# The first pass turned round: tokens stationary, split weights moving, results a token to a partition

## The chip, the cores and the metric

The kernel runs on one core of a Trainium2 chip. TensorE multiplies a stationary operand of at most 128 x 128, which it loads first, by a moving operand of up to 512 columns, and adds into a PSUM bank. VectorE (DVE), ScalarE (ACT) and GpSimd (POOL) do the work beside it, and 16 DMA engines, most of whose transfers SyncE (SP) starts, bring the weights from HBM. The metric is the device time of one execution in microseconds (us). The kernel before takes 3499.53 us (median of three runs, 3499.0 to 3501.36).

## The reference

The program computes one layer of a block on 512 tokens of 2048 channels: a norm, one combined projection, two branches (forgetting attention and multi-scale pooling), a gated merge, and then a retrieval of single-neuron experts.

```python
h = rms_norm(x, norm1_g)                              # x: 512 x 2048
q, k, v, fl, pin, gl = split(h @ w_in)                # 1024 1024 1024 8 1024 4096 columns
log_f = log_sigmoid(fl + forget_bias)
attn = forgetting_attention(rms(q), rms(k), v, log_f) # 8 heads x 128, causal
# pooling: trailing mean over 2, 4, 8 or 16 tokens minus the token itself, then a 256 x 256 map
merged = sig(gl_A) * (attn @ w_branch_attn) + sig(gl_B) * (pool * scale @ w_branch_pool)
x = x + merged @ w_out
xn = rms_norm(x, norm2_g)
s1, s2 = (xn @ w_query) @ sub_keys                    # 8 heads, 2 halves, 128 keys each
# top 16 of s1, top 16 of s2, top 16 of the 256 sums -> 16 experts a head and token
x = x + sum over the experts of gelu(u . xn) * gate * v
```

All of it is float32. TensorE takes float32 operands in two ways here. Plain float32 goes through the array in several passes. The other way splits a value into a part `hi` that has the type float32r and a rest `lo`, and forms `hi*hi + hi*lo + lo*hi` with three matmuls of one pass each.

## The kernel before

The 512 tokens are worked in two passes over the same weights, and then the experts. **Pass A** takes the first 128 tokens through norm, projection, both branches, merge, output map and query scores, so that the gathered experts of these tokens can be fetched by GpSimd during the rest. **Pass B** takes the other 384 tokens through the same layers. Last come the dense sweeps over all experts, `u` and `v`, for the first 320 of those 384.

Weights come in tiles of 128 x 2048 float32, 1 MB each, through a pool `wraw` of three buffers (line 68), loaded by SP. `plan` (lines 101 to 129) lists the tiles in the order in which they are used. An entry marked `"dve"` is split: ACT casts each half of the tile to `whi` (line 162), DVE subtracts it from the raw half to get `wlo` (line 174), and both go to a pool `wsp` of four halves each (line 69). So a `wraw` buffer of a split tile is free again when DVE has made its second `wlo`, and that of an unsplit tile when TensorE has read it. `next_w` (line 182) makes sure that the tile in use and the next one are split and that the one after is being loaded.

Pass A before uses no split. Its 112 tiles (64 of `w_in`, 16 each of the branch maps, of `w_out` and of the query map) go raw to `mm1` (line 223): for each tile 16 plain float32 matmuls, the weights stationary and 128 tokens moving, so that results come a channel to a partition:

```python
nc.tensor.matmul(ps, lhsT=raw[:, (k0 + k) * m:(k0 + k + 1) * m], rhs=x[:, k0 + k, :], ...)
```

A PSUM bank takes four such tiles side by side. The four loops of pass A are at lines 501 (projection, `order_a`), 561 (branch maps), 590 (`w_out`) and 797 (query map). I call them its four stages. Between tiles, `run_gens` runs one step of each generator in the list `gens`. The generators carry what hangs on the results: `poolA` (347), which makes the window sums by shifted adds on DVE, `forgetA` (403), `qkA_norm` (429), `attendA` (439), `tokens_a` (579) and `scores_a` (781), whose top-16 search (`topk16`, line 612) is all on DVE. `inputs_b` (535) prepares the operands `hh` and `hl` of pass B, 16 steps, during the branch stage.

Each engine works its instructions strictly in the order in which this program writes them. Pass B starts with the first `wmm` of the loop at line 969.

Of the kernel before, what the change touches and what calls it, by code (L numbers as in the profile page):

```python
# [21 lines left out]
P = 128  # L22
# [40 lines left out]
def block_kernel(ctx, tc, a):  # L63
# [37 lines left out]
    plan = []  # L101
    heads = []
    order_a = [("pin", i) for i in range(8)]
    for hb in range(2):
        order_a += [(kind, 4 * hb + i) for kind in "qkv" for i in range(4)]
        order_a += [("g", 8 * hb + i) for i in range(8)]
    order_a += [("g", i) for i in range(16, 2 * KD)]
# [7 lines left out]
    for order, eng in ((order_a, None), (order_b, "dve")):  # L115
        for kind, i in order:
            plan.append((a[src1[kind]][i], eng))
        for name in ("wbr", "wo", "wqu"):
            for i in range(KD):
                plan.append((a[name][i], eng))  # L120
# [75 lines left out]
    def next_raw():  # L196
        n = st["use"]
        st["use"] += 1
        st["split"] = st["hi"] = 2 * n + 2
        ensure_load(n + 2)  # L200
        return raws.pop(n)

    gens = []

    def run_gens():
        for g in list(gens):
            try:
                next(g)
            except StopIteration:
                gens.remove(g)  # L210

# [41 lines left out]
    xA = pA.tile([P, KD, NA], F32, name="xA")  # L253
# [6 lines left out]
    xt0 = row_tile()  # L260
    nc.scalar.dma_start(xt0, a["x"][0:P])
# [64 lines left out]
    hA = pA.tile([P, KD, NA], F32, name="hA")  # L326
    for c in range(4):
        nc.vector.tensor_tensor(hA[:, 4 * c:4 * c + 4, :], xA[:, 4 * c:4 * c + 4, :],  # L328
                                g1[:, 4 * c:4 * c + 4, None].to_broadcast([P, 4, NA]), op=OP.mult)
    nc.scalar.activation(xt0, xt0, AF.Square, accum_out=ssn[:, 0:1])  # L330
    zA = pA.tile([P, 2 * KD, NA], F32, name="zA")
    apA = pA.tile([P, KD, NA], F32, name="apA")
    es_1, p1 = lpool("p1a")
    state = {}

    def first_rstd():
        narrow_rstd(0, 1)
        state["rstdA"] = row_bcast(p1, [rsn[:, 0:1]], "rstdA")

    def scaledA(ps, out):  # L340
        nc.vector.tensor_tensor(out, quad(ps), state["rstdA"][:, None, :].to_broadcast([P, 4, NA]),
                                op=OP.mult)

    wpgA = p1.tile([P, D], F32, name="wpg")
    nc.scalar.dma_start(wpgA, a["wpg"])

    def poolA(c, ps):
        raw = p1.tile([P, 4, NA], F32, name="raw", bufs=3)
        scaledA(ps, raw)
        nc.gpsimd.tensor_copy(carry[:, 4 * c:4 * c + 4, :], raw[:, :, NA - 16:])  # L350
        yield
        for gg in range(2):
            g = 2 * c + gg
            w = WINDOWS[g]
            cur, step = raw[:, 2 * gg:2 * gg + 2, :], 1
            rw = cur
            while step < w:
                nxt = p1.tile([P, 2, NA], F32, name="pc", bufs=3)
                nc.scalar.copy(nxt[:, :, :step], cur[:, :, :step])
                nc.vector.tensor_tensor(nxt[:, :, step:], cur[:, :, step:], cur[:, :, :NA - step],  # L360
                                        op=OP.add)
# [1133 lines left out]
```

## Time and profile before

| | us |
|---|---|
| median of three runs | 3499.53 |
| the profiled execution | 3504.21 |
| its span, from the first to the last instruction | 3502.4 |
| TensorE busy | 3383.0 (97%) |
| VectorE busy | 2534.9 (72%) |
| ScalarE busy | 1360.9 (39%) |
| projection stage of pass A (64 tiles) | 11.6 to 276.0 |
| branch stage (16 tiles) | 276.0 to 333.4 |
| `w_out` stage (16 tiles) | 333.4 to 397 |
| query stage (16 tiles), end of pass A | 397 to 459.9 |

The stage borders are where the first matmul of the next stage stands in the chain of waits. A plain float32 matmul leaves two records of TensorE in this trace, so a tile of pass A shows 32. The granted clock over the run is 0.989 of 2.4 GHz. Matmuls overlap in their records: what one costs in a stream is the distance from its start to the next start, not the length of its record.

### The profile page before, as it was taken

What the parts mean: (1) busy time and instruction counts of PE and PEld (TensorE: products, weight loads), DVE (VectorE), ACT (ScalarE), POOL (GpSimd) and SP (SyncE); (2) the same over time, 40 slices, a digit from 0 to 9 for tenths busy, and PEclk for the clock granted to TensorE, in tenths of its full rate; (3) what the DMA queues carried; (4) which work ended last, traced back from release to release, by engine and by line L of the source; (5) the groups of instructions that cost most, each with busy time, mean ns of one, the idle gap of its engine ahead of it and who ended that gap; (6) DMA issues with size and microseconds to landing.
All of it is one profiled execution on the core that took longest, in us unless ns stands there. A gap on an engine that the chain in (4) does not pass through costs nothing.

```text
span 3502.4 us, 54635 instructions
## 1 busy us (share of the span) xinstructions
PE 3383.0 (97%) x22581; PEld 3329.1 (95%) x22581; DVE 2534.9 (72%) x3338; ACT 1360.9 (39%) x2067; POOL 632.7 (18%) x401
## 2 busy tenths in 40 slices
PE   8999999999998999999999998999998999999998
PEld 8999998999997999999999998999998999999997
DVE  2103287878785877887777767888887888888885
ACT  2211124555543333435467663333332333333332
POOL 0000002323231222220000002222222222222220
PEclk9999999999998999999999999999999999999999
DMA  7788876868677898774555679999998999898994
GB/s 266 284 296 317 286 265 242 319 261 319 262 292 268 340 343 322 279 275 159 196 171 178 223 271 366 359 343 360 347 347 321 363 361 352 327 369 337 366 339 155
DMA packets 228057, 1037.18 MB, mean 296 GB/s; under 512 B 21344, under 2 KB 108560, under 8 KB 114208
## 3 DMA queue, kind: packets, MB, share of 16 engines
q1 hardware_dynamic: 145792, 577.29, 44.8%
q0 software_dynamic: 55520, 402.77, 30.7%
q10 hardware_dynamic: 26496, 53.64, 4.0%
q8 instruction: 177, 2.90, 0.3%
q14 instruction: 72, 0.59, 0.0%
HBM read 980.05 MB, written 53.56 MB: 295 GB/s over the span
## 4 chain that ended last, share of the span: by engine, by line
PE 60%; issue 20%; DVE 9%; DMA 6%; ACT 4%; POOL 1%; ACTq 0%; SPq 0%; POOLq 0%; DVEq 0%
PE psm L225 10%; PE psv L216 8%; PE psv L217 8%; PE psv L215 8%; PE psm L217 8%; PE psm L216 7%; PE psm L215 7%; DVE wlo L174 2%; DMA row<-v,gidx 2%; DVE tok L735 2%; DMA wraw<-wo 1%; PE psx L216 1%; PE psx L217 1%; PE psx L215 1%; ACT h5h L1350 1%
## 5 line engine op out<-in xcount | busy, mean ns | idle before, releaser
L174 DVE TENSOR_TENSOR wlo<-wraw,whi 128x1024 fp32r<-128x1024 f32 x614 | 733.3, 1221 | 186.5 <-ACT whi L162 181.5
L162 ACT CAST whi<-wraw 128x1024 fp32r<-128x1024 f32 x614 | 638.4, 1048 | 566.5 <-PE psv L216 372.2
L217 PE MATMUL psv<-h5h,wlo 128*128 128x320 f32 x2048 | 636.2, 311 | 17.3 <-DVE wlo L174 17.3
L217 PE MATMUL psm<-xnh,wlo 128*128 128x320 f32 x2048 | 636.6, 311 | 11.7 <-DVE wlo L174 11.6
L215 PE MATMUL psm<-xnh,whi 128*128 128x320 f32 x2048 | 639.3, 312 | 6.6 <-ACT at L1318 6.1
L215 PE MATMUL psv<-h5h,whi 128*128 128x320 f32 x2048 | 636.3, 311 | 4.6 <-ACT h5h L1350 4.4
L216 PE MATMUL psv<-h5l,whi 128*128 128x320 f32 x2048 | 637.5, 311 | 1.1
L216 PE MATMUL psm<-xnl,whi 128*128 128x320 f32 x2048 | 635.2, 310 | 0.0
L695 POOL DMA_INDIRECT row<-u,gidx x133 | 238.2, 1791 | 1103.0 <-DVE row L732 606.5
L695 POOL DMA_INDIRECT row<-v,gidx x138 | 216.8, 1571 | 1159.5 <-DVE tok L735 1100.4
L217 PEld LDWEIGHTS psv<-h5h,wlo 128*128 128x128 f32 x2048 | 387.0, 189 | 18.6 <-DVE wlo L174 18.6
L217 PEld LDWEIGHTS psm<-xnh,wlo 128*128 128x128 f32 x2048 | 387.7, 189 | 13.7 <-DVE wlo L174 13.7
L215 PEld LDWEIGHTS psm<-xnh,whi 128*128 128x128 f32 x2048 | 388.1, 190 | 7.2 <-ACT at L1318 6.4
L215 PEld LDWEIGHTS psv<-h5h,whi 128*128 128x128 f32 x2048 | 386.9, 189 | 6.6 <-ACT h5h L1350 6.4
L216 PEld LDWEIGHTS psv<-h5l,whi 128*128 128x128 f32 x2048 | 386.9, 189 | 5.0 <-DVE h5l L1351 4.1
L216 PEld LDWEIGHTS psm<-xnl,whi 128*128 128x128 f32 x2048 | 388.0, 189 | 0.0
L215 PE MATMUL psm<-hh,whi 128*128 128x384 f32 x1024 | 353.7, 345 | 0.0
L217 PE MATMUL psm<-hh,wlo 128*128 128x384 f32 x1024 | 347.6, 339 | 5.1 <-DVE wlo L174 5.1
L216 PE MATMUL psm<-hl,whi 128*128 128x384 f32 x1024 | 346.8, 339 | 0.0
L735 DVE SCALAR_TENSOR_TENSOR tok<-row,gact,tok 128x2048 f32<-128x2048 f32 x138 | 323.7, 2346 | 9.3 <-DMA row<-v,gidx 8.4
L732 DVE SCALAR_TENSOR_TENSOR row<-row,tok 128x2048 f32<-128x2048 f32 x133 | 301.9, 2286 | 13.8 <-DMA row<-u,gidx 13.6
L225 PE MATMUL psm<-hA,wraw 128*128 128x128 f32 x2560 | 293.5, 277 | 12.3 <-DVE hA L328 11.6
(349 smaller groups left out, 5005.4 us busy)
## 6 DMA issues: line engine op xcount, KB each, us to landing
wraw<-uT SPq DMA_DIRECT2D x112, 1024.0 KB
wraw<-vd SPq DMA_DIRECT2D x96, 1024.0 KB
wraw<-wgl SPq DMA_DIRECT2D x55, 1024.0 KB
wraw<-wbr SPq DMA_DIRECT2D x32, 1024.0 KB
wraw<-wo SPq DMA_DIRECT2D x32, 1024.0 KB
wraw<-wqu SPq DMA_DIRECT2D x32, 1024.0 KB
xraw<-vd SPq DMA_DIRECT2D x32, 1024.0 KB
g_d<-stg ACTq DMA_DIRECT2D x10, 2048.0 KB
```

Of the source, the lines that this page charges most:

```text
L162: nc.scalar.copy(hi, raws[i][:, half * HD:(half + 1) * HD])
L174: nc.vector.tensor_tensor(lo, raws[i][:, half * HD:(half + 1) * HD], hi.bitcast(F32), op=OP.subtract)
L215: nc.tensor.matmul(ps, lhsT=wh, rhs=xh, start=first and i == 0, stop=False)
L216: nc.tensor.matmul(ps, lhsT=wh, rhs=xl, start=False, stop=False)
L217: nc.tensor.matmul(ps, lhsT=wl, rhs=xh, start=False, stop=last and i == n - 1)
L225: nc.tensor.matmul(ps, lhsT=raw[:, (k0 + k) * m:(k0 + k + 1) * m], rhs=x[:, k0 + k, :], start=k == 0, stop=k == n - 1)
L695: nc.gpsimd.indirect_dma_start(out=r, out_offset=None, in_=a[kind], in_offset=bass.IndirectOffsetOnAxis(ap=gidx[grp][:, j:j + 1], axis=0))
L732: nc.vector.scalar_tensor_tensor(r, r, 1.0, tok, op0=OP.mult, op1=OP.mult, accum_out=gact[:, j:j + 1])
L735: nc.vector.scalar_tensor_tensor(tok, r, gact[:, j:j + 1], tok, op0=OP.mult, op1=OP.add)
L1350: nc.scalar.copy(hp[0], at)
```

## The change

Pass A now works on split weights, and the operands change places. `mmA` holds the 128 tokens (`xh`, `xl`, also split) as the stationary operand and moves the weights, 512 columns at a time. A 1 MB tile now holds 512 output columns of four input blocks of 128, and four tiles make one group of 512 columns in one PSUM bank, a token to a partition. The weights of pass A are laid out anew for this (`_rows`). There are 112 tiles as before, in 28 groups, all marked `"dve"`.

With a token to a partition, the norm's factor is a number per partition (`rsn[:, 0:1]`), applied by ACT where it empties a bank. The pooling of the 128 tokens becomes a matmul with a band matrix (`bands`, 128 x 128 for each window). q and k are normed in this layout and then transposed. The merged rows, the residual rows and the query rows are transposed on TensorE before the next stage, since each stage needs its tokens' channels on the partitions, and are split again. `inputs_b` runs in the `w_out` stage now. Pass B and all that follows keep their code.

```diff
-            if plan[i][1] is None:
-                return
...
+    plan = [(a["w1A"][col1[kind] + i, q], "dve") for kind, i in groups_a for q in range(4)]
+    for name in ("wbrA", "woA", "wquA"):
+        plan += [(a[name][i, q], "dve") for i in range(4) for q in range(4)]
...
-    def mm1(ps, raw, x, k0=0, n=KD, m=P):
-        for k in range(n):
-            nc.tensor.matmul(ps, lhsT=raw[:, (k0 + k) * m:(k0 + k + 1) * m], rhs=x[:, k0 + k, :],
-                             start=k == 0, stop=k == n - 1)
+    def mmA(ps, xh, xl, q, k0, first, last, tick):
+
+        hi, lo = next_w()
+        for kk in range(4):
+            wh, wl = hi[:, kk * S:(kk + 1) * S], lo[:, kk * S:(kk + 1) * S]
+            k = k0 + kk
+            nc.tensor.matmul(ps, lhsT=xh[:, k, :], rhs=wh, start=first and kk == 0, stop=False)
+            nc.tensor.matmul(ps, lhsT=xl[:, k, :], rhs=wh, start=False, stop=False)
+            nc.tensor.matmul(ps, lhsT=xh[:, k, :], rhs=wl, start=False, stop=last and kk == 3)
+            if kk == 1:
+                tick()
...
+        nc.vector.tensor_tensor(x4, x4, g1[:, 4 * c:4 * c + 4, None].to_broadcast([P, 4, NA]),
                                 op=OP.mult)
+        nc.scalar.copy(hAh[:, 4 * c:4 * c + 4, :], x4)
+        nc.vector.tensor_tensor(hAl[:, 4 * c:4 * c + 4, :], x4,
+                                hAh[:, 4 * c:4 * c + 4, :].bitcast(F32), op=OP.subtract)
+        if c == 1:
+            ensure_split(0)
+    sq0 = row_tile()
+    nc.scalar.activation(sq0, xr0, AF.Square, accum_out=ssn[:, 0:1])
...
     def poolA(c, ps):
+        t = rowsA(ps, "raw", 3)
+        yield
+        pm, pc = bank(), bank()
+        for j in range(4):
+            nc.tensor.matmul(pm[:, j * P:(j + 1) * P], lhsT=t[:, j * P:(j + 1) * P],
+                             rhs=bands[:, 2 * c + j // 2, :], start=True, stop=True)
...
+    for n, (kind, i) in enumerate(groups_a):
+        ps = acc_bank()
+        for q in range(4):
+            mmA(ps, hAh, hAl, q, 4 * q, q == 0, q == 3, run_gens)
+            if n == 0 and q == 0:
+                narrow_rstd(0, 1)
+            ahead()
+            if q < 3:
+                after()
+        if kind == "pin":
+            gens.append(poolA(i, ps))
...
+        elif kind == "g":
+            nc.scalar.activation(zA[:, i * S:(i + 1) * S], ps, AF.Copy, scale=rsn[:, 0:1])
...
+    def mergedA(i, ga):
+        yield
+        tb = bank()
+        for j in range(4):
+            nc.tensor.transpose(tb[:, j * P:(j + 1) * P], ga[:, j * P:(j + 1) * P], ident)
+        th, tl = [t[:, 4 * i:4 * i + 4, :].rearrange("p j t -> p (j t)") for t in (mAh, mAl)]
+        nc.scalar.copy(th, tb)
+        nc.vector.tensor_tensor(tl, tb, th.bitcast(F32), op=OP.subtract)
...
+    for i in range(4):
+        kk = p3.tile([P, 2, 2 * P], F32, name="kk", bufs=2)
+        nc.scalar.dma_start(kk, a["keys"][2 * i:2 * i + 2].rearrange("h p i k -> p h (i k)"))
+        ps = acc_bank()
+        for q in range(4):
+            mmA(ps, nAh, nAl, q, 4 * q, q == 0, q == 3, run_gens)
+            ahead()
+            after()
+        gens.append(scores_a(i, ps, kk))
+        run_gens_last()
```

Three places show what this does to the order on the engines. In each row stand the line, the operation, what is written from what, and the shape; xN is a run of N equal rows.

On TensorE, the second and third groups of tiles of the projection stage. Before (`hA` are the tokens, `wraw` raw weights, `mx` pooled tokens):

```order
L225 MATMUL psm<-hA,wraw 128x128 x48
L320 MATMUL psx<-dg,ones 128x128
L225 MATMUL psm<-hA,wraw 128x128 x32
L374 MATMUL psx<-mx,wpg 128x128 x4
L225 MATMUL psm<-hA,wraw 128x128 x16
```

and now (`XH` and `XL` are the split tokens; the end of the first half of the fifth tile, and then the pooling):

```order
L223 MATMUL psm<-whi,XH 128x512
L224 MATMUL psm<-whi,XL 128x512
L225 MATMUL psm<-wlo,XH 128x512
L373 MATMUL psx<-bands,raw 128x128 x4
L376 MATMUL psx<-ident,raw 128x16 x4
L223 MATMUL psm<-whi,XH 128x512
```

A tile was 16 matmuls of 128 columns and is 12 of 512, and each now needs a `whi` or a `wlo`.

On ScalarE, the start of the program. Before:

```order
L330 ACT_TABLE_LOAD
L330 ACTIVATE row,ssn<-row 128x2048
L345 DMA wpg<-wpg 128x2048
L302 ACT_TABLE_LOAD
L302 ACTIVATE rsn<-ssn 128x1
```

and now (the square of the 128 token rows is L341):

```order
L335 CAST XH<-xA 128x512 x2
L156 CAST whi<-wraw 128x1024
L335 CAST XH<-xA 128x512 x2
L341 ACTIVATE row,ssn<-xr_94 128x2048
L346 DMA wpg<-wpg 128x2048
L156 CAST whi<-wraw 128x1024 x3
L305 ACT_TABLE_LOAD
```

The cast of the second half of the first weight tile stands behind the square, which waits for the token rows.

On VectorE, the query stage, between two searches (`cf` are the 256 sums of a head, `s` its scores). Before:

```order
L623 MAX_INDEX ix_2385<-v_2531,s_2510 128x8
L644 TENSOR_TENSOR cf<-v_2530,v_2531 128x256
L614 MAX tops<-cf 128x8
L616 MAX_INDEX pos<-tops,cf 128x8
L618 MATCH_REPLACE cf<-tops,cf 128x256
L621 MAX tops<-cf 128x8
L623 MAX_INDEX pos<-tops,cf 128x8
L614 MAX v_2567<-s_2510 128x8
```

and now:

```order
L679 MAX_INDEX ix_2844<-v_3033,s_3008 128x8
L168 TENSOR_TENSOR wlo<-wraw,whi 128x1024 x2
L700 TENSOR_TENSOR cf<-v_3032,v_3033 128x256
L670 MAX tops<-cf 128x8
L672 MAX_INDEX pos<-tops,cf 128x8
L674 MATCH_REPLACE cf<-tops,cf 128x256
L677 MAX tops<-cf 128x8
L679 MAX_INDEX pos<-tops,cf 128x8
L670 MAX v_3073<-s_3008 128x8
```

The searches of pass A had VectorE to themselves and now share it, in strict order, with the splitting of the weights.

## Rows read from the trace of the kernel before

**Rows 1.** The page's first part: busy time, share of the span, instructions

```profile
PE 3383.0 (97%) x22581; PEld 3329.1 (95%) x22581; DVE 2534.9 (72%) x3338; ACT 1360.9 (39%) x2067; POOL 632.7 (18%) x401
```

**Rows 2.** Windows: us; busy PE, PEld, DVE, ACT, POOL; granted clock, DMA share, GB/s

```profile
11.00:276.00 265.00, 252.06 (x2179) 246.77 (x2180) 42.76 (x95) 52.84 (x94) 0.98 (x2) 1.00 0.80 282
276.00:333.00 57.00, 57.00 (x512) 56.95 (x511) 23.84 (x41) 8.67 (x17) 0.00 (x0) 1.00 0.92 338
333.00:397.00 64.00, 60.00 (x529) 59.15 (x528) 5.99 (x9) 3.93 (x9) 0.00 (x0) 1.00 0.85 283
397.00:460.00 63.00, 61.60 (x550) 61.25 (x549) 32.59 (x152) 10.69 (x16) 0.00 (x0) 1.00 0.86 291
...
468.00:474.00 6.00, 0.96 (x6) 0.64 (x4) 5.83 (x25) 1.52 (x2) 0.00 (x0) 0.78 0.83 344
474.00:482.00 8.00, 7.91 (x34) 7.91 (x35) 7.93 (x8) 1.05 (x1) 0.00 (x0) 0.74 0.70 259
...
2900.00:3100.00 200.00, 197.26 (x1327) 195.90 (x1327) 171.33 (x181) 69.03 (x87) 49.67 (x34) 0.99 0.92 348
```

**Rows 3.** Chain of waits in pass A: start us, us, what

```profile
18.30 7.34 DMA wraw<-wpin
...
68.62 14.31 PE psm L225 x128
...
276.02 57.36 PE psm L225 x512
333.40 7.42 DMA wraw<-wo
...
383.58 9.62 DMA wraw<-wo
...
451.16 4.90 DMA wraw<-wgl
```

**Rows 4.** Timeline of TensorE, attention of pass B: start us, us, engine, line

```profile
611.87 0.39 PE L215 MATMUL psx<-n1h,n0h 128*128 128x512 f32 x1
612.10 0.40 PE L216 MATMUL psx<-n1l,n0h 128*128 128x512 f32 x1
612.34 0.40 PE L217 MATMUL psx<-n1h,n0l 128*128 128x512 f32 x1
```

**Rows 5.** Timeline of ScalarE at the start

```profile
17.36 1.91 ACT L330 ACTIVATE row<-row 128x2048 f32<-128x2048 f32 x1 [12.29 <-DMA row<-x]
```

**Rows 6.** The page's fifth part, splitting: busy us, mean ns

```profile
L174 DVE TENSOR_TENSOR wlo<-wraw,whi 128x1024 fp32r<-128x1024 f32 x614 | 733.3, 1221 | 186.5 <-ACT whi L162 181.5
L162 ACT CAST whi<-wraw 128x1024 fp32r<-128x1024 f32 x614 | 638.4, 1048 | 566.5 <-PE psv L216 372.2
```

**Rows 7.** Groups by line on VectorE, pass A: busy us, mean ns, idle before

```profile
L549 DVE SCALAR_TENSOR_TENSOR xB<-xB,g,rstdB 128x384 f32<-128x384 f32 x16 | 9.8, 614 | 8.0 <-DMA xB<-xB 8.0
L553 DVE TENSOR_TENSOR hl<-xB,hh 128x384 fp32r<-128x384 f32 x16 | 8.9, 557 | 6.9 <-ACT hh L551 6.9
...
L571 DVE TENSOR_TENSOR zA<-zA,psm 128x512 f32<-128x512 f32 x4 | 2.8, 690 | 14.7 <-PE psm L225 14.7
```

**Rows 8.** Timeline of VectorE: the first instruction of two searches in a row

```profile
448.32 0.49 DVE L614 MAX8 v<-s 128x8 f32<-128x128 f32 x2 [4.75 <-ACT s L792]
...
453.50 0.47 DVE L614 MAX8 v<-s 128x8 f32<-128x128 f32 x2
```

**Rows 9.** Timeline of TensorE where pass B starts: idle time in brackets

```profile
459.92 0.42 PE L215 MATMUL psm<-hh,whi 128*128 128x384 f32 x1
...
474.09 0.69 PE L217 MATMUL psm<-hh,wlo 128*128 128x384 f32 x1 [5.13 <-DVE wlo L174]
```

**Rows 10.** Chain of waits there, matmuls of 384 columns: start us, us

```profile
475.10 0.32 PE psm L216
...
478.65 0.18 PE psm L216
```

More of the change, by code (lines that the diff above doesn't have):

```diff
@@ new lines, in poolA @@
+        pm, pc = bank(), bank()
[3 more added lines that the diff above has]
+        for j in range(4):
+            nc.tensor.matmul(pc[:, j * 16:(j + 1) * 16], lhsT=t[:, j * P:(j + 1) * P],
+                             rhs=ident[:, P - 16:], start=True, stop=True)
+        m = p1.tile([P, 4, NA], F32, name="mx", bufs=2)
+        nc.scalar.copy(m.rearrange("p j t -> p (j t)"), pm)
@@ L405, in forgetA @@
         ps = bank()
-        mm1(ps[:H, :NA], fraw, hA, m=H)
-        log_forget(p1, ps, NA, 0, state["rstdA"], ccA, 0.0, ("fz", "fe", "fu", "fl"))
+        for k in range(KD):
+            nc.tensor.matmul(ps[:, :H], lhsT=xA[:, k, :], rhs=fraw[:, k * H:(k + 1) * H],
+                             start=k == 0, stop=k == KD - 1)
+        fl = p1.tile([P, H], F32, name="fr")
+        nc.scalar.activation(fl, ps[:, :H], AF.Copy, scale=rsn[:, 0:1])
+        yield
+        pt = bank()
+        nc.tensor.transpose(pt[:H, :NA], fl, ident)
+        log_forget(p1, pt, NA, 0, ccA, 0.0, ("fz", "fe", "fu", "fl"))
+        yield
         yield
@@ L429, in qkA_norm @@
     def qkA_norm(which, hb, ps):
-        raw = p1.tile([P, 4, NA], F32, name="raw", bufs=3)
-        scaledA(ps, raw)
+        t = rowsA(ps, "raw", 3)
+        v = p1.tile([P, 12], F32, name="hv", bufs=2)
+        sq = p1.tile([P, S], F32, name="sqA")
+        for j in range(4):
+            nc.scalar.activation(sq[:, j * P:(j + 1) * P], t[:, j * P:(j + 1) * P], AF.Square,
+                                 accum_out=v[:, j:j + 1])
+        nc.vector.tensor_scalar(v[:, :4], v[:, :4], 1.0 / P, EPS, op0=OP.mult, op1=OP.add)
+        rsqrt_nr(v[:, 4:8], v[:, :4], v[:, 8:])
+        yield
+        nc.vector.tensor_tensor(quad(t), quad(t), v[:, 4:8, None].to_broadcast([P, 4, P]), op=OP.mult)
+        yield
+        pt = bank()
+        for j in range(4):
+            nc.tensor.transpose(pt[:, j * P:(j + 1) * P], t[:, j * P:(j + 1) * P], ident)
         out = p1.tile([P, 4, NA], F32, name="n%d" % which)
+        nc.scalar.activation(out.rearrange("p j t -> p (j t)"), pt, AF.Copy,
+                             scale=(kg if which else qg)[:, 0:1])
         qkA[which, hb] = out
-        yield from head_norm(p1, raw.rearrange("p j t -> p (j t)"), S, kg if which else qg,
-                             out.rearrange("p j t -> p (j t)"), "sc", 4)
         if which:
@@ new lines, in block_kernel, with sigmoids @@
+    for g in list(gens):
+        for _ in g:
+            pass
+    gens.clear()
+    es_1.close()
+    mAh = pA.tile([P, KD, NA], F32R, name="XH")
+    mAl = pA.tile([P, KD, NA], F32R, name="XL")
+    def sigmoids(i):
+        for z in (zA[:, i * S:(i + 1) * S], zA[:, D + i * S:D + (i + 1) * S]):
+            nc.scalar.activation(z, z, AF.Sigmoid)
+        yield
+    def mergedA(i, ga):
+        yield
+        tb = bank()
+        for j in range(4):
+            nc.tensor.transpose(tb[:, j * P:(j + 1) * P], ga[:, j * P:(j + 1) * P], ident)
+        th, tl = [t[:, 4 * i:4 * i + 4, :].rearrange("p j t -> p (j t)") for t in (mAh, mAl)]
+        nc.scalar.copy(th, tb)
+        nc.vector.tensor_tensor(tl, tb, th.bitcast(F32), op=OP.subtract)
@@ L529, in block_kernel @@
+    for _ in range(2):
+        run_gens()
+    es_z.close()
     es_h, ph = rpool("ph")
@@ L786, in scores_a @@
             norm_a()
+        pt = bank()
+        for j in range(4):
+            nc.tensor.transpose(pt[:, j * P:(j + 1) * P], qt[:, j * P:(j + 1) * P], ident)
+        qa = quad(p3.tile([P, S], F32, name="scr", bufs=2))
+        nc.scalar.copy(qa.rearrange("p j t -> p (j t)"), pt)
+        yield
         pss = bank()
```

284 lines of the change are left out of this document (121 added, 163 removed).

## The prediction

> **What bounds the kernel now.** I read the busy times first, then windows cut at the borders of pass A's stages, then the chain of waits, then single operations. The busy times show TensorE at 97% of the span and VectorE at 72% [rows 1]: TensorE sets the time nearly everywhere, and the dense part after pass A leaves it no slack (197.26 of 200 us busy, DMA at 0.92 [rows 2]). So what pass A saves or loses before 460 us arrives at the end nearly one for one, since everything behind keeps its order and its bound. Within pass A the windows show TensorE busy for 252 of 265, 57 of 57, 60 of 64 and 61.6 of 63 us, VectorE for 43, 24, 6 and 33, ScalarE for less than 53, and the DMA engines at 0.80 to 0.92 [rows 2]. In the chain 64 plain float32 matmuls (128 records, four tiles) take 14.31 us and the branch stage is one row of 57.36 us [rows 3]: 3.58 us a tile. The reader is to see two things: TensorE is the bound, and DMA stands close behind it, while VectorE and ScalarE have room in the first three stages and less in the fourth.
>
> **The change part by part.**
>
> *Matmuls.* Three matmuls of 512 columns in a row start 0.23 and 0.24 us apart [rows 4], so one costs 0.235 us in a stream, and a tile of 12 costs 2.82 us instead of 3.58. For 112 tiles that is 316 us instead of 401: 85 us is the most that TensorE can give. The small float32 matmuls (pooling by the band, transposes instead of the norm's sums) I cost at nothing, because TensorE is no longer the bound: a dozen to three dozen in a stage at 0.11 to 0.22 us (14.31 us for 64 [rows 3]) are 2 to 8 us, and TensorE waits longer than that in each stage by the sums below. If that cover were gone they would cost these few us.
>
> *Splitting.* 224 halves are cast and subtracted, 1.048 us each on ScalarE and 1.221 us on VectorE [rows 6]: 2.10 and 2.44 us a tile, below the 2.82, but in strict order with everything else on those engines.
>
> *Weights.* The bytes stay. A tile is 1.049 MB; with the DMA engines fully busy it would take 2.86 us by the branch stage's window (338 GB/s at 0.92), 3.15 by the `w_out` stage's (283 at 0.85) and 2.77 by the late one (348 at 0.92) [rows 2]. In the projection stage 64 tiles share the engines with some 5.5 MB of token rows, pool weights and stored keys and values, which gives 3.0 to 3.4 us a tile. So DMA passes TensorE as the bound.
>
> *Buffers.* Three `wraw` buffers remain, but each is now held by another user: from the issue of its load until the second `wlo`. After landing that is two casts and one subtraction, 3.3 us, with hand-offs about 3.5. The landings that the chain shows take 4.90 to 9.62 us [rows 3]; they are the late ones, and many others must be under 7.2 us, two tiles' time, for TensorE never waits in the branch stage. One buffer's round is thus 8.4 to 13.1 us, a tile's third of it 2.8 to 4.4. I take 3.3 us a tile, a landing of 6.4 us, between the earliest and the middle of the rows; it also lies inside the DMA bound.
>
> *Start.* Before, the fourth load is issued at 18.30 and lands 7.34 us later [rows 3], since TensorE frees the first buffer. Now the second half of the first tile is cast only behind the square of the token rows, which begins at 17.36 and takes 1.91 us and a short read [rows 5]: 19.5, then 1.05 and 1.22 for the split, so 21.7; the fourth tile lands at about 29. The 60 tiles behind it follow at 3.3 us, and the last needs 5 us to be split and used: the projection stage ends at 29 + 198 + 5 = 232 us, where it was 276.
>
> *Branch stage.* VectorE needs 16 x 2.44 = 39.1 us for the split and four groups of four operations on 512 elements at 0.69 [rows 7], 11.0: 50.1. The loads need 16 x 3.3 = 53 and are late last. At its end TensorE waits about 2 us for the last products before it can transpose them: 55 us, against 57.
>
> *`w_out` stage.* `inputs_b` is moved here: 16 times 0.614 and 0.557 us on VectorE [rows 7], 18.7; its eight loads of 0.39 MB go through SP's queue between the weights. With 39.1 for the split and 12 operations at 0.69, 8.3, VectorE needs 66 us, DMA 60 (16 tiles, these loads and 1 MB of stores, at 3.0), TensorE 45. VectorE is late last; with 2 us of hand-offs 68, against 64.
>
> *Query stage.* One search takes 5.18 us (453.50 less 448.32 [rows 8]). The program order puts five and a half of the eight searches ahead of the last weights of this stage: 28.5 and 39.1, so 67.6 us, with 2 of hand-offs 69, against 63. TensorE waits behind VectorE here, up to 5.2 us at a time, where one search's second half and the next one's first half stand together between two pairs of `wlo`. What such waits may do to its clock is weighed with the rivals.
>
> *Start of pass B.* Before, TensorE used up the first split tile, waited 5.13 us for a `wlo` behind the last searches [rows 9], and the next 13 matmuls ran 0.32 us apart instead of 0.175 [rows 10]: 7 us. Now one and a half tiles of pass B are split ahead of those searches, 12.6 us of matmuls at 0.175, and the last two and a half searches take 13.0, beside some 3 us of query work that TensorE still does first. I count the 7 us as gained; bounds 0 and 7.
>
> *Sum.* 232 + 55 + 68 + 69 = 424 for the start of pass B, which was 459.9 [rows 9]: 36 us, and 7 behind it, 43. The profiled execution took 3504.2 (span 3502.4 and 1.8 around it), so it would take 3461; it lies 4.7 above the median of the runs, so I forecast 3457.
>
> **The rivals.**
>
> *TensorE stays the bound where VectorE is not (3430).* If loads land in 5.5 us, the round is 9.0 and a tile costs 3.0, with TensorE's 2.82 and its small work equal. Then the projection ends at 214, the branch stage takes 50, the others 66 and 67.6: 398, which is 62 and 7 us. For it: 4.90 [rows 3] and 378 GB/s at full share late on [rows 2]. Against it: only 333 to 367 in pass A's own windows.
>
> *Slower: the three buffers turn too slowly (3520).* This is the round of a `wraw` buffer, in all 112 tiles: landing plus 3.5 us, over three. TensorE used to give a buffer back without the split. Loads that land in 9.1 us make it 4.2 us a tile: 29 + 108 x 4.2 + 5 = 488, later than before by 28, less 7. It decides from 4.0 us a tile, a landing of 8.5 us. For it: loads of 7.42 and 9.62 us with two tiles in flight [rows 3]. Against it: the branch stage took a tile each 3.58 us with landings under 7.2 and DMA at 0.92 without a wait [rows 2].
>
> *TensorE falls to half its clock (3484).* After the wait of 5.13 us the granted clock was 0.78 and 0.74 of full in the mean of two windows [rows 2], and the spacing 0.32 instead of 0.175 us shows the lower level, 1.2 GHz [rows 10]; the waits of the `w_out` stage, 4 us in 64, left it at 1.00 [rows 2]. At 1.2 GHz a tile takes 512/384 x 0.32 x 12 = 5.1 us. If the two stages that VectorE bounds run so, they take 82 us each instead of 68 and 69: 27 less of gain, 16 left. If all of pass A did, it would end beyond 600 and the run near 3640; the many short waits of the first two stages speak against that. The Trainium skill has this as a rule (TensorE: Matmul & The Clock Gate, "HAM oscillation — how this bites in real kernels"): where each weight tile's matmuls are shorter than the wait for the next one, the array starts every tile at half its clock. This trace agrees for the one long wait and not for the short ones.
>
> **How the numbers follow.** Forecast 0.58, TensorE bound 0.17, slow buffers 0.14, half clock 0.11. A difference under 0.2%, 7 us, is no change for a measurement of this kernel. The forecast's own range is 3437 to 3480 (3.0 to 3.6 us a tile in the first two stages, pass B's start unchanged or better). The first two cases are faster, as is most of the third's weight near 3484; slow buffers between 3.8 and 4.0 us a tile would be no change: faster 0.83, same 0.06, slower 0.11. The range that should hold 8 in 10 goes to 3418, a little under the second case, and to 3505, where the slow buffers begin to cost; above it stand most of that case and the full half clock.
>
> **What would show it.** Right: rows of 512 columns 0.23 us apart; the first matmul of pass B at 400 to 445 us; a tile each 3.0 to 3.6 us in the projection stage, TensorE idle there behind `wlo` or `whi` and these behind DMA, which stands at 0.9 or more; VectorE busy for over 90% of the last two stages; no idle of 5 us at pass B's start; windows from 520 us on as before, only shifted. Wrong: loads that land over 8.5 us after issue; a granted clock well below 1.00 in pass A; ScalarE, which empties the banks in order with its casts, as the releaser of most of TensorE's idle time; or a stretch after pass A that has become longer.

## The result, and the profile after

The changed kernel takes 3523.55 us (median of 4 runs, 3519.59 to 3526.73), beside 3499.27 for the kernel before: a ratio of 1.0068, 95% interval [1.005, 1.0085]. It is slower by 0.7%, and 3457 was forecast. Its profiled execution has a span of 3517.8 us, where it was 3502.4.

The first part of its page answers to [rows 1]. TensorE is busy for 52 us less, VectorE for 250 and ScalarE for 232 more; this is the shape that was forecast.

```profile
PE 3331.4 (95%) x20404; PEld 3195.4 (91%) x20404; DVE 2784.9 (79%) x3572; ACT 1592.7 (45%) x2339; POOL 633.5 (18%) x399
```

The windows of the kernel after, columns as in [rows 2], cut where TensorE begins the projection, branch, `w_out` and query stages and pass B, then ten microseconds in pass B's start and a stretch of the dense part:

```profile
15.00:268.00 253.00, 216.62 (x922) 168.93 (x923) 176.22 (x220) 181.19 (x252) 0.00 (x0) 0.94 0.76 286
268.00:322.00 54.00, 47.51 (x211) 37.21 (x209) 48.98 (x50) 40.80 (x47) 0.00 (x0) 1.00 0.87 333
322.00:403.00 81.00, 58.80 (x213) 40.64 (x211) 56.57 (x73) 41.24 (x57) 0.00 (x0) 0.92 0.64 248
403.00:478.00 75.00, 58.68 (x246) 46.06 (x247) 68.10 (x170) 44.06 (x54) 0.00 (x0) 0.90 0.73 267
492.00:502.00 10.00, 5.74 (x22) 5.71 (x22) 9.79 (x17) 0.58 (x1) 0.00 (x0) 0.66 0.49 174
2900.00:3100.00 200.00, 197.83 (x1343) 196.69 (x1341) 170.67 (x184) 68.90 (x88) 50.40 (x33) 1.00 0.90 341
```

In the first row no engine is full: TensorE 217 of 253 us, VectorE 176, ScalarE 181, the DMA engines at 0.76. Where nothing is full, the time lies in waits between engines. Pass B starts at 477.5 us instead of 459.9, and the last instruction comes 15.4 us later than before: what pass A loses arrives at the end, as the forecast had it. Against the forecast the stages stand so:

| | forecast | after | difference |
|---|---|---|---|
| end of projection stage | 232 | 268.2 | +36 |
| branch stage | 55 | 53.7 | -1 |
| `w_out` stage | 68 | 81.0 | +13 |
| query stage | 69 | 74.6 | +6 |
| start of pass B | 424 | 477.5 | +53.5 |

So two terms have to be explained, the projection and the `w_out` stage. The waits of the kernel after in the projection stage, 30 to 262 us (engine, line, what it waited for, us in total, times, longest):

```profile
DVE wlo L168 <- ACT whi L156: 37.4, 43, 3.3
PEld psm L225 <- DVE wlo L168: 30.0, 23, 5.0
ACT whi L156 <- DMA wraw<-w1A: 29.5, 20, 3.7
PE psm L225 <- DVE wlo L168: 21.5, 14, 4.6
SPq L146 <- DVE wlo L168: 147.3, 46, 8.1
```

Each engine waits for the one ahead of it: TensorE for the subtraction, VectorE for the cast, ScalarE for the load. And SyncE's loads (last row) wait for VectorE to free a buffer. That is a ring, and none of its rows says who holds it up. The issues of the same kernel in 30 to 262 us (count, KB, median us from issue to landing) rule out one suspect at once: weights land in 4.9 us, earlier than the forecast's 6.4 and far from the slow rival's 9.1.

```profile
wraw<-w1A SPq DMA_DIRECT2D x59, 1024.0 KB, 4.9
```

The timeline of ScalarE and VectorE in the kernel after, at the head norm of q (start us, us), shows one lump in the ring:

```profile
93.59 1.05 ACT L156 CAST whi<-wraw 128x1024 fp32r<-128x1024 f32 x1 [0.83 <-DMA wraw<-w1A]
94.63 0.69 ACT L365 ACTIVATE raw<-psm,rsn 128x512 f32<-128x512 f32 x1
95.35 0.31 ACT L455 ACTIVATE sqA<-raw 128x128 f32<-128x128 f32 x1
...
96.65 1.28 ACT L305 ACT_TABLE_LOAD   x1
...
98.17 1.28 ACT L306 ACT_TABLE_LOAD   x1
...
99.58 2.93 ACT L156 CAST whi<-wraw 128x1024 fp32r<-128x1024 f32 x3
```

From 94.63 to 99.58 us ScalarE empties a bank, squares four heads and loads its function tables twice, 5 us without a cast; behind them three casts wait. The Trainium skill (ScalarE activation tables: per-element evaluation and per-set limits, "What a function is on this engine") gives 1283 ns for a change between sets, and this trace has 1283 ns for each. TensorE runs dry and idles for 3.69 us, until 101.46. The windows around that place, same columns as above:

```profile
94.00:102.00 8.00, 4.31 (x18) 3.29 (x17) 2.60 (x7) 7.91 (x17) 0.00 (x0) 0.96 0.56 229
102.00:106.00 4.00, 4.00 (x15) 3.09 (x14) 3.41 (x4) 1.60 (x3) 0.00 (x0) 0.64 0.57 188
106.00:118.00 12.00, 11.86 (x57) 9.60 (x55) 7.10 (x7) 7.40 (x9) 0.00 (x0) 1.00 0.96 356
```

After the idle time the granted clock is 0.64, a mixture of the levels 1.2 and 2.4 GHz, and 1.00 again behind it. So a lump costs TensorE the idle time and then some time at half clock. The Trainium skill (TensorE: Matmul & The Clock Gate, "HAM oscillation — how this bites in real kernels") says that a burst of matmuls behind a long enough wait starts at half clock; the trace agrees.

### The profile page after: what moved, and what is told of

Same layout as the page of the kernel before. It is cut to its first block, busy times and chain, and to the rows that moved or that the text cites. A ratio compares the mean times of both kernels' runs of the same rounds, so it can differ in the third digit from the quotient of the medians.

```text
span 3517.8 us, 51131 instructions
## 1 busy us (share of the span) xinstructions
PE 3331.4 (95%) x20404; PEld 3195.4 (91%) x20404; DVE 2784.9 (79%) x3572; ACT 1592.7 (45%) x2339; POOL 633.5 (18%) x399
## 4 chain that ended last, share of the span: by engine, by line
PE 50%; issue 22%; DVE 14%; ACT 7%; DMA 6%; POOL 1%; ACTq 0%; SPq 0%; DVEq 0%; POOLq 0%
PE psv L210 8%; PE psv L211 8%; PE psv L209 7%; PE psm L211 7%; PE psm L209 7%; PE psm L210 7%; DVE wlo L168 5%; DVE tok L791 2%; ACT whi L156 2%; DMA wraw<-w1A 2%; DMA row<-v,gidx 2%; PE psm L225 1%; ACT h5h L1401 1%; PE psx L210 1%; PE psx L211 1%
## 5 line engine op out<-in xcount | busy, mean ns | idle before, releaser
L168 DVE TENSOR_TENSOR wlo<-wraw,whi 128x1024 fp32r<-128x1024 f32 x838 | 997.6, 1221 | 257.0 <-ACT whi L156 254.9
L156 ACT CAST whi<-wraw 128x1024 fp32r<-128x1024 f32 x838 | 863.4, 1048 | 618.1 <-PE psv L210 371.4
L156 ACT CAST whi<-xraw 128x1024 fp32r<-128x1024 f32 x122 | 127.6, 1047 | 162.1 <-PE psv L210 143.2
```

The source lines that it names most:

```text
L168: nc.vector.tensor_tensor(lo, raws[i][:, half * HD:(half + 1) * HD], hi.bitcast(F32), op=OP.subtract)
```

## The experiments

All ratios are to the kernel before, run beside. Stage lengths in the experiments are read from the end of the split of a stage's last weight tile to that of the next; in the kernel after they are 242.5 us (tile 0 to 63), 49.9 (to 79), 84.1 (to 95) and 70.4 us (to 111).

### e1: the chains cut into steps

```diff
-        nc.vector.tensor_scalar(v[:, :4], v[:, :4], 1.0 / P, EPS, ...)
-        rsqrt_nr(v[:, 4:8], v[:, :4], v[:, 8:])
         yield
+        nc.vector.tensor_scalar(v[:, :4], v[:, :4], 1.0 / P, EPS, ...)
+        nc.scalar.activation(v[:, 4:8], v[:, :4], AF.Ln)
+        nc.scalar.activation(v[:, 4:8], v[:, 4:8], AF.Exp, scale=-0.5)
+        yield
...
```

> The changed kernel with the same work, but the chains between VectorE and ScalarE in pass A (norm of q and k, forget gate) cut into more steps, one a weight tile, so that neither engine waits for the other inside a step. Theory (lumps in order): the split of the weights stands on both engines behind these chains, and the six gaps of 5.6 to 11.4 us between finished tiles around them are the loss, some 30 us over a pace of 3 us; the projection stage falls from 253 us to about 235 and the run from 3523 to about 3505. Rival (three buffers and the landing of loads set the pace): projection stage stays at 250 or more, run within 5 us of 3523.

Measured: 3520.68 us, 1.0057 [1.004, 1.0074]; projection stage 245.5 us. The cut gave nothing. The waits within a step do not set the stage.

### e2: the inputs' loads on another queue

```diff
-            nc.sync.dma_start(xs[c]...
+            nc.gpsimd.dma_start(xs[c]...
```

> The changed kernel, with the eight loads of xB put on GpSimd's queue instead of SyncE's. Theory (a load that waits for its buffer holds back the weights queued behind it): in the w_out stage weights come in pairs each 10.7 us; without that the stage is bound by VectorE, 66 to 68 us instead of 74, and the run gains about 7 us. Rival (the hand-over between VectorE and ScalarE over hh and hl sets the pace of that stage): stage within 2 us of 74, no gain.

Measured: 3519.38 us, 1.0055 [1.0039, 1.0072]; `w_out` stage 83.3 us, as it was. SyncE's queue is not what holds it up.

### e3: a fourth buffer of loaded weights

```diff
+    es_r, pr1 = rpool("pr1")
+    extra["raws"] = pr1
...
+        if n == 15:
+            extra["raws"] = None
```

> The changed kernel with a fourth buffer for raw weight tiles during the projection stage. Rival of the prediction (the round of three buffers sets the pace, 3.95 us a tile): with four the pace falls to 3.0 and the stage from 253 us to about 200 to 215. Theory (lumps in order on ScalarE and VectorE): the tiles have landed and wait to be split, so the stage loses 8 us at most.

Measured: 3510.89 us, 1.0032 [1.0022, 1.0042]; projection stage 233.9 us. The 8.6 us are close to the theory's 8: the buffers matter, but do not set the pace.

### e4: no head norm

```diff
-        for j in range(4):
-            nc.scalar.activation(sq[...], t[...], AF.Square, accum_out=v[:, j:j + 1])
-        nc.vector.tensor_scalar(v[:, :4], v[:, :4], 1.0 / P, EPS, ...)
-        rsqrt_nr(v[:, 4:8], v[:, :4], v[:, 8:])
...
-        nc.vector.tensor_tensor(quad(t), quad(t), v[:, 4:8, None]..., op=OP.mult)
```

> The changed kernel without the norm of q and k of the first 128 tokens (squares, root and scaling are left out; the transposes stay): it prices those four chains. Theory (lumps in order): the four gaps of 5.6 to 8.5 us at the q and k groups go, 18 to 22 us off the projection stage and as much off the run. Rival (buffers and landing): within 5 us of 3523, since these chains are under 10% of what ScalarE and VectorE do there.

Measured: 3501.76 us, 1.0007 [0.9997, 1.0016]; projection stage 221.8 us. The stage is 20.7 us shorter, 5.2 for each of the four lumps. Three of them take 5 us as the one above, the first, with one table load, takes 4, and the bank is still emptied in this run: between the splits of tile 0 and tile 63 ScalarE is busy for 15 us less and VectorE for 4. So the lumps are paid in full, in a stage where ScalarE is idle for 72 of 253 us.

### e5: the inputs of the `w_out` stage one step ahead

The timeline of one tile in that stage of the kernel after shows what the edit is about:

```profile
336.52 0.55 DVE L621 TENSOR_TENSOR hl<-xB,hh 128x384 fp32r<-128x384 f32 x1
336.99 0.61 DVE L617 SCALAR_TENSOR_TENSOR xB<-xB,g,rstdB 128x384 f32<-128x384 f32 x1
337.64 0.51 ACT L619 CAST hh<-xB 128x384 fp32r<-128x384 f32 x1 [2.47 <-DVE xB L617]
338.06 1.99 ACT L156 CAST whi<-wraw 128x1024 fp32r<-128x1024 f32 x2
339.13 2.36 DVE L168 TENSOR_TENSOR wlo<-wraw,whi 128x1024 fp32r<-128x1024 f32 x2 [1.52 <-ACT whi L156]
341.40 0.55 DVE L621 TENSOR_TENSOR hl<-xB,hh 128x384 fp32r<-128x384 f32 x1
```

ScalarE's cast `hh` waits 2.47 us for VectorE's scaling, then VectorE waits 1.52 us for the next `whi`; the period is 341.40 less 336.52, 4.9 us, where VectorE has 3.5 us of work. In 322 to 403 us the first of these waits alone comes to 35 us:

```profile
ACT hh L619 <- DVE xB L617: 35.4, 15, 2.5
DVE wlo L168 <- ACT whi L156: 20.5, 16, 2.1
```

```diff
-                nc.vector.scalar_tensor_tensor(xs[c][:, j, :], ...)
-                nc.scalar.copy(hh[:, k, :], xs[c][:, j, :])
+            nc.scalar.copy(hh[:, k, :], x)
+            if k + 1 < KD:
+                scaled(k + 1)
                 yield
```

> Edit: in the w_out stage the scaling of x's block k+1 (VectorE) is put one step ahead of the cast of block k (ScalarE), so that within a step neither engine waits for the other's result of the same step. Same operations, same loads. Theory (the stage is a strict alternation of ScalarE and VectorE, 4.9 to 5.6 us a tile, and not the larger sum of the two): the stage goes from 84 us to about 67 (VectorE's 53 us busy plus start and end), the run by about 15 us, to 3508. Rival (the stage waits for weights landing): the same instructions wait for the same loads, the stage stays at 80 to 86 and the run at 3520 to 3524.

Measured: 3513.06 us, 1.004 [1.0027, 1.0052]; `w_out` stage 76.1 us. Half of what was expected. The alternation is gone from the waits of e5 in 320 to 395 us, and a wait for late weights has come:

```profile
DVE wlo L168 <- ACT whi L156: 13.9, 12, 3.2
PEld psm L223 <- ACT whi L156: 11.8, 6, 3.1
ACT whi L156 <- DMA wraw<-woA: 11.0, 5, 4.4
```

### e6: the root on VectorE

```diff
-        rsqrt_nr(v[:, 4:8], v[:, :4], v[:, 8:])
+        nc.vector.memset(v[:, 4:8], 0.25)
+        for _ in range(6):
+            nc.vector.scalar_tensor_tensor(v[:, 8:], v[:, 4:8], -0.5, v[:, 4:8], ...)
...
```

> Edit: the inverse root of the head norms of the first 128 tokens is taken on VectorE by six Newton steps from a constant start, without ScalarE's Ln and Exp and their two table loads; the four squares stay on ScalarE. It takes about 3.0 us off ScalarE four times and puts about 2.9 us on VectorE four times. Theory (it is ScalarE's time in order that is added in full, VectorE has some left): the projection stage goes from 242.5 us by 10 to 12 us to about 231, the run to about 3512. Rival (any lump on either engine counts alike, since the three buffers turn through both): stage within 3 us of 242, run 3519 to 3524.

Measured: 3525.12 us, 1.0061 [1.0048, 1.0074]; projection stage 246.4 us, 3.9 more than in the kernel after where the rival allowed 3. ScalarE is busy for 8 us less in the stage and VectorE for 10 more. So the rival was right in kind: ScalarE's time is not special, and a lump on either engine of the ring counts about alike.

### e7: a longer lead of the split

```diff
-            hi = wsp.tile([P, HD], F32R, name="whi")
+            hi = half_tile("whi")
...
-        ensure_split(2 * n + 3)
+        ensure_split(2 * n + (3 if extra.get("halves") is None else 5))
```

In the projection stage `half_tile` takes every third half from two more buffers.

> Edit: in the projection stage six halves of each split weight instead of four, and the split runs one tile further ahead of TensorE; the three buffers of loaded weights stay. Theory (no slack: the lumps of ScalarE's time are added in full because the split leads by 1.5 tiles only): with 2.5 tiles of lead a lump of 5 us is partly worked off, ScalarE being busy 181 of 253 us: the stage goes to 220 to 230, B starts 12 to 20 us earlier, the run at 3503 to 3512. Rival (the loop of three loaded buffers through ScalarE and VectorE sets 2.97 us a tile, and the lumps come on top of it whatever the lead): the stage stays at 238 to 244, the run at 3518 to 3524.

Measured: 3524.97 us, 1.0073 [1.0061, 1.0085]; projection stage 244.6 us. No gain, but the wait has moved. The first waits of e7 in 30 to 240 us that bear on TensorE:

```profile
PE psx L472 <- DVE raw L468: 22.2, 4, 6.9
DVE wlo L174 <- ACT whi L162: 19.9, 27, 2.0
PEld psx L472 <- ACT whi L162: 17.3, 3, 7.3
```

TensorE hardly waits for `wlo` any more but, four times, for the normed rows that it is to transpose. With a longer lead VectorE's multiplication of the norm stands behind more splits, and TensorE, which takes its instructions in order, stands at the transposes with split weights ready.

### e8: three edits at once

The edit joins the fourth buffer (e3), the root on VectorE (e6) and the inputs one step ahead (e5).

> Edit: three at once, the fourth buffer of loaded weights in the projection stage (8.6 us by itself), the root on VectorE and the inputs of the w_out stage one step ahead. Theory: the three act on different things and add up, 8.6 + 11 + 15 = 35 us, so about 3488, which would be faster than the kernel before (3499.5). Rival (they relieve the same engines, and what one gives back the next bound takes): 3500 to 3512.

Measured: 3503.89 us, 1.0007 [0.9998, 1.0015]: 20 us less than the kernel after, where e3 (13) and e5 (10) make 23 between them. So nothing is left for the root on VectorE, though this run does not separate the three.

### e9: later transposes

This is e7 with one more edit:

```diff
         nc.vector.tensor_tensor(quad(t), quad(t), v[:, 4:8, None]..., op=OP.mult)
         yield
+        yield
+        yield
         pt = bank()
```

> Edit: the six halves and the longer lead of e7, and in the norm of q and k the transposes on TensorE two steps later (three weight tiles after the norm's last VectorE operation is issued instead of one). Theory (the lumps are worked off by a lead, but TensorE takes its instructions in order, and in e7 the four idle stretches of 4.6 to 6.9 us stand before the transposes of the normed rows, which hold up the matmuls behind them): the four gaps, 22 us, go nearly all, the stage ends 15 to 20 us earlier than in e7, B starts at 460 to 466, the run at 3502 to 3510. Rival (the sum of ScalarE's work and the loop of loads sets the pace in any case, the gap only moves to the next wait): B starts at 476 to 482, the run at 3519 to 3525.

Measured: 3524.73 us, 1.0063 [1.005, 1.0077]; projection stage 247.5 us. The rival was right: the waits for normed rows went, and ScalarE's waits for loads rose to 34 us in 30 to 240, from 24.5 in the kernel after. A lead on the split's side alone is worth nothing.

### e10, e11 and e12: queue, sum, and chains with a lead

e10 is e5 with e2's queue; e11 is e9 with e10 and the pooling's first matmuls one step later; e12 is e11 with e1's cut.

> Edit: the inputs of the w_out stage one step ahead (e5) and their loads on GpSimd's queue (e2). Theory (with the alternation gone, the next wait in e5 is for weights, ScalarE's 11 us <- DMA woA, issued late because they stand in SyncE's queue behind a load of inputs that waits for its buffer): the stage goes from e5's 76 to 66 to 70 us, the run from 3513 to about 3505. Rival (the weights are late because their own buffer comes free late): the stage stays at 74 to 78, the run at 3511 to 3515.

> Edit: e9 and e10 together, and the pooling's first matmuls one step later. Theory (slack in both stages; the two add up): 3524 less 17 (projection) less 18 (w_out stage), about 3488, faster than the kernel before by 0.3%. Rival (they do not add up): 3500 or more.

> Edit: e11, and the norm's chain of ScalarE and VectorE cut into one step a tile (e1). Theory: with a lead, the 10 us in which VectorE waits inside the norms for ScalarE are no longer hidden by nothing, and the cut gives 3 to 8 us more than e11: about 3483. Rival (e1 gave nothing, and the lead already covers these waits): equal to e11 within 3 us.

Measured: e10 3519.8 us, 1.0054 [1.0041, 1.0068], `w_out` stage 82.0 us, worse than e5: on their own queue the inputs come late instead, VectorE waits 14 us for them. e11 3517.57, 1.0046 [1.0032, 1.0059]: its theory fell with e9's and e10's. e12 3513.7, 1.0032 [1.002, 1.0043]: less than e11 by 4 us of medians, the size that its theory gave this step, though the intervals overlap. Both runs lie 30 us above their forecasts.

### e13, e14 and e17: which side of the split lacks slack

e17 has more buffers for loads, e13 has these and e9's lead, and e14 loads half of each tile. First the edit of `raw_tile` in e13 and e17, then that of the load in e14:

```diff
-        if extra["raws"] is not None and extra["raw"] % 4 == 0:
-            return extra["raws"].tile([P, D], F32, name="xraw")
+        i = extra["raw"]
+        if i <= 36:
+            if i % 6 == 4:
+                return prow.tile([P, D], F32, name="tok")
+            if i % 6 in (5, 0):
+                return prow.tile([P, D], F32, name="row", bufs=2)
+        elif i <= 62:
+            if i % 4 == 0:
+                return prow.tile([P, D], F32, name="tok")
```

```diff
+            if i < 64:
+                nc.sync.dma_start(raw[:, :HD], plan[i][0][:, :HD])
```

> Edit: e9 (six halves, a longer lead, later transposes), and more buffers for loaded weights in the projection stage: six up to weight tile 36, four up to tile 62, in row buffers that the stage does not use then. Theory (during a lump the three loaded buffers are full and the loading stops, and afterwards loading at 2.97 us a tile is hardly faster than TensorE takes tiles, so neither a longer lead alone (e7, e9: nothing) nor one buffer alone (e3: 8.6 us) gives the lump back; both sides together do): the stage goes from 242.5 to 215 to 225 us, its first half most, B starts at 452 to 462, the run at 3494 to 3503. Rival (ScalarE's own order sets the stage, its work and its waits, whatever the buffers): the stage stays at 232 to 244, the run at 3510 to 3524.

> Edit: each of the 64 weight tiles of the projection stage is loaded by half only, and both halves of the split are made from the loaded half, so the other half of w_in's columns is left out of the computation; everything else as in the changed kernel. Theory (loading stops during a lump and cannot catch up): with half the bytes a tile lands in about 3 us and the loading catches up at once; the stage goes from 242.5 to 218 to 228 us. Rival (the split's engines set the pace, loads are early enough): the stage stays at 236 to 243.

> Edit: the buffers of loaded weights of e13 (six up to weight tile 36, four up to 62) without its six halves, longer lead and later transposes. Theory (slack is needed on both sides of the split): the stage goes to 231 to 235 us, as with one buffer more (e3, 234) and with half the bytes (e14, 233), and not to e13's 221. Rival (buffers for loads are all that is needed): 220 to 225 us.

Measured, projection stage and run: e17 232.3 us, 3524.75 us, 1.0054 [1.0038, 1.0071]; e14 232.7 us, 3508.69 us, 1.0022 [1.0011, 1.0032]; e13 221.0 us, 3512.0 us, 1.0032 [1.0021, 1.0043]. The window of e14 from 15 to 245 us, and its first waits in 30 to 230:

```profile
15.00:245.00 230.00, 201.66 (x859) 159.26 (x860) 166.03 (x210) 172.37 (x242) 0.00 (x0) 0.93 0.47 159
```

```profile
PEld psm L230 <- DVE wlo L173: 23.4, 18, 4.1
DVE wlo L173 <- ACT whi L160: 23.3, 31, 2.8
PE psm L230 <- DVE wlo L173: 17.0, 10, 3.7
```

The same window and the first waits of e13:

```profile
15.00:245.00 230.00, 203.50 (x898) 162.80 (x899) 171.13 (x217) 176.34 (x249) 0.00 (x0) 0.96 0.80 308
```

```profile
DVE wlo L181 <- ACT whi L169: 10.9, 14, 2.8
DVE hv L322 <- ACT hv L321: 10.2, 4, 2.9
PEld psm L238 <- DVE wlo L181: 8.8, 7, 3.7
```

e14 frees the loads altogether (DMA share 0.47) and gains 10 us, as e17 does with more buffers. TensorE still waits 17 to 23 us for `wlo`, since a lump of 5 us is longer than its lead of one and a half tiles, 4.2 us. Lead alone gave nothing (e7, e9), buffers alone 10 us, both 21.5: the theory of two missing slacks holds. Of the 10 us of e17 and the 21.5 of e13, 3 are no gain: there, as in e15 and e16, the first tile is split at 26.9 us instead of 23.9, since the square ahead of it waits 2.9 us for token rows that land later beside more early loads. Counted from the start of the span, the last split of the stage comes 7 us earlier in e17, 10 in e14 and 18 in e13. The order of the four cases stays.

The theory also fits e7 and e9. In the late half of the kernel after, 180 to 230 us, the DMA engines move 363 GB/s at a share of 0.92, so they need 2.9 us for a tile of 1.049 MB, and TensorE 2.8. The engines can do more: with more buffers, e13 moves 422 GB/s from 182 to 216 us, 2.5 us a tile. But three buffers and landings of 4.9 us give 2.8 us a tile at best, by the forecast's own sum, (4.9 + 3.5) / 3. That is an estimate, and by it loading that stops during a lump cannot catch up with TensorE. The two windows, the kernel after and e13:

```profile
180.00:230.00 50.00, 44.12 (x191) 34.35 (x190) 34.58 (x36) 37.03 (x47) 0.00 (x0) 0.97 0.92 363
182.00:216.00 34.00, 28.26 (x122) 23.08 (x121) 24.10 (x24) 27.44 (x37) 0.00 (x0) 0.90 1.01 422
```

The runs of e13 and e17 show less than their stages for a second reason: both lose 6 to 7 us far behind, between the same two splits of the dense sweeps (at 2644 and 2765 us in the kernel after). e15 and e16, which use the same buffers, lose as much there; e3, e4 and e5 do not. The two lines that the diff above takes out gave the kernel after a fourth buffer of loaded weights behind pass A, too: its trace has 61 loads into `xraw`, 13 in pass B and 48 in the dense sweeps, and the traces of e13, e15, e16 and e17 have none. Around the place of the loss ScalarE waits longer for weights, first in the kernel after (2640 to 2780 us), then in e16 (2600 to 2740 us):

```profile
ACT whi L156 <- DMA wraw<-vd: 27.9, 2, 20.2
ACT whi L169 <- DMA wraw<-vd: 36.2, 4, 26.5
```

So these four runs are each the wanted edit and a lost buffer, and their times understate what the slack in pass A is worth. No run puts the buffer back alone; that it is the cause of the loss is read from the edits and the traces, not tested.

### e15 and e16: slack in the projection stage, and throughout

e15 is e13 with e1's cut, e5's inputs and the pooling's first matmuls one step later; e16 adds:

```diff
-        elif i <= 62:
+        elif i <= 108:
...
         nc.vector.tensor_tensor(pr, pr, sm[:, :, 1:2].to_broadcast([P, 4, NA]), op=OP.mult)
         yield
+        yield
+        yield
```

> Edit: e13, the norms' chains and the pooling's first step cut into one step a tile (e12), and the inputs of the w_out stage one step ahead (e5). Theory: e13's 22 us, 4 us of the chains as between e11 and e12, and e5's 9 us: about 3488, faster than the kernel before by 0.3%. Rival (they relieve the same engine): 3500 to 3510.

> Edit: e15, with the fourth buffer of loaded weights kept on to weight tile 108, so through the branch, w_out and query stages, and two more steps before the attention's and the forget gate's transposes. Theory (the w_out stage, 76 us, and the query stage, 75 us, wait 27 us for weights that land late, and the projection stage 11 us for two transposes): w_out stage to 70, query stage to 70, projection stage to 215 to 218, together 12 to 17 us less than e15: about 3488, faster than the kernel before by 0.2 to 0.4%. Rival (what one stage gives back the next takes): 3499 to 3503, the same as before.

Measured: e15 3502.59 us, 1.0001 [0.9992, 1.001], as its rival had it; e16 3486.14 us, 0.9955 [0.9941, 0.9968]. e15's stages are 222.3, 50.2, 75.6 and 75.3 us; what the projection gains is paid in part by a `w_out` and a query stage that wait for weights. With the fourth buffer kept through pass A, e16's are 216.9, 47.9, 67.7 and 67.6, and it is the fastest of all, faster than the kernel before by 0.45%. Its windows, cut at TensorE's borders as those of the kernel after:

```profile
15.00:247.00 232.00, 211.74 (x923) 167.28 (x924) 176.39 (x222) 180.55 (x253) 0.00 (x0) 0.96 0.82 320
247.00:296.00 49.00, 46.16 (x206) 36.69 (x205) 45.74 (x48) 39.76 (x45) 0.00 (x0) 1.00 0.91 351
296.00:362.00 66.00, 55.69 (x216) 42.44 (x217) 57.92 (x73) 42.43 (x58) 0.00 (x0) 0.90 0.83 302
362.00:433.00 71.00, 55.74 (x241) 43.65 (x240) 65.51 (x167) 42.41 (x51) 0.00 (x0) 0.93 0.71 262
```

The work in the first row is that of the kernel after, engine by engine (TensorE 212 and 217 us, VectorE 176 and 176, ScalarE 181 and 181), in 232 us instead of 253. Pass B starts at 433.3 us, 26.6 earlier than in the kernel before; the run is 15 us faster, with the dense sweeps' loss of 6.5 in it.

## Why the prediction was wrong

*Matmuls.* Right. Three rows of the kernel after, of 512 columns, begin 0.23 us apart, as in [rows 4]:

```profile
330.15 0.39 PE L223 MATMUL psm<-whi,XH 128*128 128x512 f32 x1
330.38 0.40 PE L224 MATMUL psm<-whi,XL 128*128 128x512 f32 x1
330.61 0.40 PE L225 MATMUL psm<-wlo,XH 128*128 128x512 f32 x1
```

*Splitting.* The durations were right, 1.046 and 1.222 us. That they lie "in strict order with everything else on those engines" was written down and then given no price. This is the step that failed, together with the next.

*Buffers, 3.3 us a tile.* It measured 242.5 us for 63 tiles, 3.85. The forecast took a tile's round as landing plus two casts and one subtraction, 6.4 and 3.5 us over three. Both halves were off, in opposite directions. Landings took 4.9 us, which by the same sum gives 2.8 us a tile. Three times 3.85 less 4.9 leaves 6.6 us for the split with its waits, an estimate, where the forecast had 3.5. ScalarE's other 51 us in the stage (181 busy less 130.5 of casts), which the forecast hid behind DMA, were not all hidden. e4 shows that the head norms among them cost their full length, e13 and e17 that most of this is for lack of slack on both sides of the split.

*Start.* Right within 2 us: the first tile was split at 23.9 us, 21.7 forecast.

*Branch stage.* 53.7 us, 55 forecast; right.

*`w_out` stage, 68 us.* It measured 81. The forecast took the largest sum of one engine's work, VectorE's 66 us, and 2 of hand-offs as the stage's length. VectorE was busy for 57 us, so the sum was 9 too large, and the waits were 24 us, not 2, because `inputs_b` makes ScalarE and VectorE wait for each other within each step (e5) and the weights then land late (e5, e16). With both mended, in e16, the stage takes 65.4 us between TensorE's borders, and VectorE is busy for 58 of them: an engine's work is the floor, not the time. That 65.4 is near the forecast's 66 is chance.

*Query stage, 69 us.* 74.6 measured, VectorE busy for 68 of it. The term had the right engine and its work, 67.6, and allowed 2 us of waits where 6.5 were.

*Start of pass B, 7 us gained.* Not gained. TensorE idles for 4.26 us there and then runs at half clock (window 492 to 502 above, 0.66), as in [rows 9, 10]. From tile 111's split to tile 113's it takes 25.4 us in the kernel after: the searches stand between the two halves of one tile, and a lead of one and a half tiles does not reach over them.

*The rivals.* The slow one came closest in time, 3520, by luck, for its cause was wrong: its landings of 9.1 us measured 4.9. What held the buffers was not the load but the wait for ScalarE and VectorE. The half clock was a part of the truth, as a consequence: in the window 15 to 268 us the mean clock is 0.94, so at most 6% of 253 us, 15 us, can go there, an estimate, after the idle times that the lumps make. With VectorE as bound of the last two stages it was not a cause by itself: e16's clock there is 0.90 and 0.93, and the stages take 65 and 72 us. That TensorE stays the bound was wrong: its 3.0 us a tile measured 3.85, and even in e16, with TensorE busy for 212 of 232 us and part of them at half clock, 3.44 (216.9 us for 63 tiles).

*The sum.* Of 53.5 us too early a start of pass B, 36 stand in the projection stage. e16 gives back 44 us, 21 of them there, 16 in the `w_out` stage, 4 in the branch and 3 in the query stage, and pass B starts 9 us behind the forecast's 424.

## What to carry to other kernels

Where one engine's product feeds the next through a few buffers, the largest sum of one engine's work is a floor. In this ring a lump was paid in full until there were buffers both ahead of the split and behind it; count the lead in microseconds and set it against the longest lump in the queue, not against the mean. And look for two engines that wait for each other within one step: in e5 moving one operation a step ahead was worth 8 us of 84. Last, after an edit of where buffers come from, count the loads of each buffer in the far part of the trace, which the edit was not meant to touch.

## What was not expected of the hardware

Six and later four buffers for loads let weights be asked for earlier, and they land later: 7.0 us in e13's and e16's first 245 us for those in the old buffers, 4.9 in the kernel after, while e16's projection stage moves 320 GB/s instead of 286. This fits a landing time that is partly the queue ahead, where a load that lands later may be one that was asked for earlier; no run separates it from other causes.

```profile
wraw<-w1A SPq DMA_DIRECT2D x36, 1024.0 KB, 7.0
tok<-w1A SPq DMA_DIRECT2D x12, 1024.0 KB, 6.4
row<-w1A SPq DMA_DIRECT2D x11, 1024.0 KB, 5.2
```

The three rows are e16's issues in 15 to 245 us. And moving small loads to GpSimd's queue, meant to relieve SyncE's, made the `w_out` stage 6 us longer in e10 than in e5; without e5's edit it changed nothing (e2).
